# Operand sums beside other products, sums' transfers in two bundles, another order of tables, loads and banks

## The chip, the core and the metric

The kernel runs on one core of a Trainium2 chip. Its engines work side by side, each on its own list of instructions: TensorE (PE) for matrix products into PSUM, VectorE (DVE), ScalarE (ACT) and GpSimd (POOL) for everything between, SyncE (SP) for issuing transfers; POOL issues transfers too. The metric is the time on the device from start to end of one execution, in microseconds, as a median over runs.

## The reference

Two layers, on 512 tokens (S) of width 1024 (D). Each layer mixes the tokens along four branches and then runs a gated feed-forward block:

```python
for l in range(2):
    h = rms_norm(x, g_pre_mix[l])
    # h @ w_in gives all projections: FOX q,k,v and forget gate; dilated q,k,v;
    # retention q,k,v and gate; latents cq (256), ckv (128), kr (32)
    o_a = causal_block_attention(fq, fk, fv, decay=cumsum(log_sigmoid(ff + b_forget)))
    o_b = dilated_attention(dq, dk, dv)
    o_c = silu(rg) * group_norm(retention(rope(rq), rope(rk), rv)) * ret_gn_gain
    o_d = causal_block_attention(MLA: rms_norm(cq) @ w_uq, rms_norm(ckv) @ w_ukv, rope(kr))
    gates = sigmoid(h @ w_gate)                       # 4 x 1024 columns
    merged = sum over the four branches of (o_n @ w_branch[n]) * gates[n]
    x = x + rms_norm(merged @ w_out, g_post_mix)
    h = rms_norm(x, g_pre_ffn)
    x = x + rms_norm((silu(h @ w_ffn_gate) * (h @ w_ffn_up)) @ w_ffn_down, g_post_ffn)
```

The feed-forward width is 2816, 22 blocks of 128. All is float32.

## The kernel before

Activations lie with the features on the 128 partitions and the 512 tokens along the row. A float32 product is made of three faster ones: both operands are split into a high and a low part, and high x high, high x low and low x high are added in PSUM (`mm3`, L528 to L530). The high part of a weight is a cast by ACT (L289, L403), the low part a subtraction by DVE (L290, L404). Weights come from HBM in 512 KB pieces on SP's queue (L258) into three `raw` buffers. Activations are split by `split_to` (L520 the cast, L521 the subtraction; L523 and L524 where a scale goes with it).

PSUM has eight banks in two rotating sets of four, "acc" and "b"; a product takes the next bank of its set, and waits until what was in that bank has been read. SBUF tiles for activations, `a`, rotate in the same way.

The order of the instructions is made at build time. Most of a layer is written as generators, one for the main stage and a list of background ones, and a scheduler then orders each engine's list; only the first block, the ends of the two blocks and the start of a layer (`ordered(True)` to `ordered(False)`) keep the order in which they are written.

A layer runs: `latents` (the four token tiles of cq, ck and the forget gate lie in the four "acc" banks, while the first half of the `dq` product runs in a "b" bank; DVE then reads the latents out at L1213 to L1217); `project` (all projections, with `mla_prepare` and the attentions in the background: transposes of the latents at L893 and L899, then K and Q from `uq` and `ukv`, which are loaded at L872 and L873); `gates`; `out_block`; `ffn`; and between the layers `down_block`.

`gates` goes through the branches; for each it makes the eight gate tiles in four pairs (`dp`): DVE scales (L1299), ACT takes the tanh (L1300), DVE multiplies with the branch's product (L1319), and from the second branch on POOL adds the result to `merged` (L1320). For the last branch (`gi == 3`) `merged` is then split for `out_block`. In the same place `make_sums` starts transfers on POOL's queue that add blocks of the last weight matrix in DRAM: p = a21 + a22, r = a11 + a21, q = p + a11, v = q + a12. Each sum is a copy and an adding transfer, and each waits for the landing of the one that it builds on. A 1x1 transfer from the gate tile holds them back until the gate is there (L360).

`ffn` makes the first four of the 22 blocks (`m`) plainly, then nine groups of two in `quarter_products`: seven products in place of eight, from quarters of the operands, each group in four banks of one set, the sets taking turns. In the last layer `to_tokens` turns the residual to token order in the background (L1726 transposes into "b", L1729 copies out).

`finish` is the last layer's down projection, again seven products (`n` = 0 to 6) in place of eight. Their right operands are the weight blocks and sums, streamed; the left ones are quarters of the hidden tiles `h` or their sums: t1 = difference of halves, t2, t3 and t4 (L1753, L1757, L1783, L1790), each made for 11 blocks of 128. Operands are made three steps ahead (`OPS`), weights two steps (`AHEAD`). The last steps of a product (`k >= LATE`) are held and run for the first bank, then for the second, so that the first can be read out (`after`: copy L1837, adds, square L1815, root L551) while the second fills. Products 0, 4, 5 and 6 share the banks `chain`. The operands of a product are made by

```python
products = (plain(0, h0), plain(FH, h0), of_t1, plain(FH, h1), of_t2, of_t3, of_t4)
beside = {1: make_t1, 3: make_t2}
```

where `of_t3` and `of_t4` compute the sum when the operand is due, and `beside` names what is computed step by step during another product.

## Time and profile before

| | us |
|---|---|
| median of 3 runs | 1693.74 |
| lowest and highest | 1692.67, 1696.91 |
| the profiled execution | 1688.88 |
| its span, first to last instruction | 1687.1 |
| PE busy | 1650.9 |
| DVE, ACT, POOL busy | 1132.2, 851.2, 376.1 |
| mean granted clock of PE | 0.997 |

The span is the time from the first to the last instruction; 1.8 us lie outside of it. "Busy" counts instructions in work, not those that wait. The ends of matrix products are modelled, and neighbouring products overlap in the records: a 512-column product is shown with 0.39 us and the next begins 0.23 us after it. The gap in front of an instruction, and what ended it, is therefore the surest reading.

### The profile page before, as it was taken

Reading aid. Unit: us, or ns where it says so; the run is one execution under the profiler, and the core shown is the slowest. Engines: PE = TensorE matmul, PEld = TensorE weight load, DVE = VectorE, ACT = ScalarE, POOL = GpSimd, SP = SyncE. Lnnn points to the kernel's source line nnn. Section 1 sums busy time; section 2 is a strip of 40 time slices with the busy share of each in tenths; the row PEclk is TensorE's granted clock in tenths of the full one; section 3 lists DMA queues with packets and bytes.
Section 4 is the critical chain, followed back from the end, with each engine's and each line's share of the span. In section 5 each row is a group of like instructions: output and inputs, shape, how many; then the busy total and the mean of one; then the engine's idle time right before and its main releaser. Section 6 shows DMA issues by size and latency. Waiting matters only on the chain.

```text
span 1687.1 us, 26433 instructions
## 1 busy us (share of the span) xinstructions
PE 1650.9 (98%) x9746; PEld 1460.2 (87%) x9746; DVE 1132.2 (67%) x2149; ACT 851.2 (50%) x1680; POOL 376.1 (22%) x404
## 2 busy tenths in 40 slices
PE   9999999999999999999999999999999999999997
PEld 7788888888798999988887888888888989999875
DVE  6667777644569777762286577675445687777987
ACT  6566553323455555553265665533334565555664
POOL 0145333332230000000121453334332300010000
PEclk9999999999999999999999999999999999999998
DMA  5644325776625777343236343257755257775561
GB/s 198 178 107 127 93 82 185 171 191 157 201 82 146 182 184 183 101 152 101 76 128 181 104 130 90 84 176 179 192 142 174 65 150 193 184 186 150 189 238 68
DMA packets 93313, 248.88 MB, mean 148 GB/s; under 512 B 11136, under 2 KB 22656, under 8 KB 93184
## 3 DMA queue, kind: packets, MB, share of 16 engines
q1 hardware_dynamic: 72768, 205.24, 38.8%
q0 software_dynamic: 20416, 41.95, 13.4%
q8 instruction: 77, 1.26, 0.3%
q14 instruction: 52, 0.43, 0.1%
HBM read 220.93 MB, written 31.46 MB: 150 GB/s over the span
## 4 chain that ended last, share of the span: by engine, by line
PE 59%; DVE 5%; ACT 2%; issue 1%; DMA 1%; POOL 1%; DVEq 0%; SPq 0%; ACTq 0%
PE acc L528 8%; PE acc L529 8%; PE acc L530 8%; PE acc L502 4%; PE acc L504 4%; PE acc L503 4%; PE b L504 3%; PE b L503 3%; PE b L502 3%; PE b L1889 1%; PE b L1891 1%; PE b L1890 1%; PE b L751 1%; DVE wlo L290 1%; PE b L671 1%
## 5 line engine op out<-in xcount | busy, mean ns | idle before, releaser
L528 PE MATMUL acc<-a,whi 128*128 128x512 f32 (+1 forms) x1238 | 477.8, 386 | 3.0 <-DVE a L1299 3.0
L530 PE MATMUL acc<-a,wlo 128*128 128x512 f32 (+1 forms) x1238 | 469.0, 379 | 0.0
L529 PE MATMUL acc<-a,whi 128*128 128x512 f32 (+1 forms) x1211 | 458.6, 379 | 0.0
L290 DVE TENSOR_TENSOR wlo<-raw,whi 128x512 fp32r<-128x512 f32 (+3 forms) x398 | 279.0, 732 | 134.1 <-ACT whi L289 133.3
L289 ACT CAST whi<-raw 128x512 fp32r<-128x512 f32 (+3 forms) x398 | 213.0, 576 | 305.8 <-PE acc L529 155.9
L530 PEld LDWEIGHTS acc<-a,wlo 128*128 128x128 f32 x1238 | 233.0, 188 | 44.0 <-issue 0.5
L528 PEld LDWEIGHTS acc<-a,whi 128*128 128x128 f32 x1238 | 233.9, 189 | 42.5 <-ACT whi L289 3.8
L529 PEld LDWEIGHTS acc<-a,whi 128*128 128x128 f32 x1211 | 228.5, 189 | 38.9 <-DVE a L524 0.6
L404 DVE TENSOR_TENSOR wlo<-raw,whi 128x1024 fp32r<-128x1024 f32 x132 | 157.6, 1195 | 71.2 <-ACT whi L403 67.7
L403 ACT CAST whi<-raw 128x1024 fp32r<-128x1024 f32 x132 | 135.4, 1027 | 122.7 <-PE acc L503 51.1
L502 PE MATMUL acc<-a,whi 128*128 128x256 f32 x560 | 158.6, 283 | 1.9 <-DVE a L1638 1.5
L503 PE MATMUL acc<-a,whi 128*128 128x256 f32 x560 | 158.4, 283 | 0.0
L504 PE MATMUL acc<-a,wlo 128*128 128x256 f32 x560 | 158.3, 283 | 0.0
L502 PE MATMUL b<-a,whi 128*128 128x256 f32 x448 | 126.8, 283 | 0.0
L503 PE MATMUL b<-a,whi 128*128 128x256 f32 x448 | 126.8, 283 | 0.0
L504 PE MATMUL b<-a,wlo 128*128 128x256 f32 x448 | 126.8, 283 | 0.0
L1299 DVE TENSOR_TENSOR a<-acc,a 128x512 f32<-128x512 f32 x64 | 44.1, 689 | 111.4 <-PE acc L530 111.4
L520 ACT CAST a<-a 128x512 fp32r<-128x512 f32 (+1 forms) x143 | 77.6, 567 | 74.7 <-DVE a L859 18.0
L333 POOL DMA_DIRECT2D raw<-wts x36 | 31.6, 877 | 350.1 <-DMA raw<-wts 129.0
L502 PEld LDWEIGHTS acc<-a,whi 128*128 128x128 f32 x560 | 107.4, 192 | 2.3 <-ACT whi L403 1.7
L503 PEld LDWEIGHTS acc<-a,whi 128*128 128x128 f32 x560 | 107.5, 192 | 0.1
L504 PEld LDWEIGHTS acc<-a,wlo 128*128 128x128 f32 x560 | 107.4, 192 | 0.0
(280 smaller groups left out, 3237.7 us busy)
## 6 DMA issues: line engine op xcount, KB each, us to landing
raw<-wts SPq DMA_DIRECT2D x257, 512.0 KB, 3.9
raw<-wts POOLq DMA_DIRECT2D x36, 512.0 KB, 6.5
a<-a SPq DMA_DIRECT2D x120, 128.0 KB, 2.3
sums<-wts POOLq DMA_DIRECT2D x30, 512.0 KB, 7.3
raw<-sums SPq DMA_DIRECT2D x20, 512.0 KB, 3.9
raw<-wts SPq DMA_DIRECT2D x35, 256.0 KB, 2.9
sums<-sums POOLq DMA_DIRECT2D x10, 512.0 KB, 4.6
a<-xT SPq DMA_DIRECT2D x16, 256.0 KB, 5.4
```

Of the source, the lines that this page charges most:

```text
L289: todo.append(lambda hi=hi, src=src, n=n: nc.scalar.copy(hi[:, :n], src))
L290: todo.append(lambda hi=hi, lo=lo, src=src, n=n: (lo_engine or nc.vector).tensor_sub(lo[:, :n], src, hi[:, :n].bitcast(F32)))
L403: self.nc.scalar.copy(hi, src)
L404: self.nc.vector.tensor_sub(lo, src, hi.bitcast(F32))
L502: mm(o, hi[:, c], x[k][0], start=first, stop=False, skip_group_check=i in (2, 3, 4, 6))
L503: mm(o, hi[:, c], x[k][1], start=False, stop=False, skip_group_check=i in (2, 3, 4, 6))
L504: mm(o, lo[:, c], x[k][0], start=False, stop=k == 3, skip_group_check=i in (2, 3, 4, 6))
L520: nc.scalar.copy(hi, src)
L528: mm(out, w[0], x[0], start=start, stop=False)
L529: mm(out, w[0], x[1], start=False, stop=False)
L530: mm(out, w[1], x[0], start=False, stop=stop)
L1299: nc.vector.tensor_mul(z, ps, self.rB)
```

## The change

- `make_sums` takes the names of the sums: p and r start at the first pair of gates, q and v at the third. Each sum now has its own 1x1 transfer ahead of it.
- For the last branch DVE, not POOL, adds to `merged`.
- `uq` and `ukv` are loaded at the beginning of `latents`. Both halves of the `dq` product go to "acc", except the one that runs beside the latents. A dummy exponential follows the latents, the forget gate's functions are computed where `running_sum` needs them, and three empty scheduling steps (`yield`) are added.
- In `down_block` two weight subtractions move from step `EA` to step 1.
- The groups of quarter products begin with "b" instead of "acc", and `finish` swaps its sets too.
- In `finish`, t3 is made beside product 2 and t4 beside product 4, as whole tiles; t4 overwrites t2.

```diff
--- before.py
+++ after.py
@@ -346,18 +346,19 @@
         return [self.ap["wts"][self.woff[i + j]:self.woff[i + j + 1]].rearrange("(p n) -> p n", p=128)
                 for j in range(len(LAST_K))]
 
-    def make_sums(self, j, when):
+    def make_sums(self, j, names, when):
 
         dma = self.nc.gpsimd.dma_start
         a11, a12, a21, a22 = (self.block_quarter(n)[j] for n in range(4))
         n = a11.shape[1]
         for name, first, more in (("p", a21, a22), ("r", a11, a21), ("q", None, a11), ("v", None, a12)):
+            if name not in names:
+                continue
             d = self.dram.tile([128, n], F32, tag="%s%d" % (name, j), name="sums")
             self.sums[name, j] = d
             if first is None:
                 first = self.sums["p" if name == "q" else "q", j]
-            else:
-                dma(d[0:1, 0:1], when[0:1, 0:1])
+            dma(d[0:1, 0:1], when[0:1, 0:1])
             dma(d, first, max_dma_last_dim=1024)
             dma(d, more, accum_op=ALU.add, max_dma_last_dim=1024)
 
@@ -849,6 +850,8 @@
         yield
         yield
         yield
+        yield
+        yield
         rb = self.ps("b")
         for t in range(4):
             ts = slice(128 * t, 128 * t + 128)
@@ -866,14 +869,9 @@
     def mla_prepare(self, l, cq, ck, res):
         nc = self.nc
         ident = self.con("ident")
-        uq_raw = [self.a(), self.a()]
-        ukv_raw = self.a()
-        for k in range(2):
-            nc.sync.dma_start(uq_raw[k], self.ap["uq"][l, :, k, :])
-        nc.sync.dma_start(ukv_raw, self.ap["ukv"][l])
-        uq = [self.split(t) for t in uq_raw]
-        yield
-        ukv = self.split(ukv_raw)
+        uq = [self.split(self.up.pop(0)) for _ in range(2)]
+        yield
+        ukv = self.split(self.up.pop(0))
         for p in range(2):
             c = ck[p][:, 0:384].rearrange("p (t c) -> p t c", t=2)
             cs = slice(64 * p, 64 * p + 64)
@@ -914,6 +912,7 @@
                 for p in range(2):
                     self.move(K[h][p][64:128, :], K[0][p][64:128, :])
         self.defer(shared)
+        yield
         yield
         Q = []
 
@@ -1185,6 +1184,9 @@
         cq, ck = [self.a(), self.a()], [self.a(), self.a()]
         z = self.small(16)
         junk = self.a()
+        self.up = [self.a() for _ in range(3)]
+        for t, src in zip(self.up, (self.ap["uq"][l, :, 0, :], self.ap["uq"][l, :, 1, :], self.ap["ukv"][l])):
+            nc.sync.dma_start(t, src)
         w = self.take("dq", 0)
         ps_d = self.ps("b")
         for k in range(KT):
@@ -1225,7 +1227,8 @@
         nc = self.nc
         cq, ck, z, ps_d = self.latents(l, u)
         yield
-        nl = self.forget(z)
+
+        nc.scalar.activation(self.small(1), z[:, 0:1], AF.Exp, scale=0.0)
         self.br = {n: {} for n in range(4)}
         m = {"qk": [], "v": []}
         self.bg.append(("mprep", self.mla_prepare(l, cq, ck, m)))
@@ -1235,7 +1238,7 @@
             q, k, v = [], [], []
             for i in range(2):
                 if ps_d is None:
-                    ps_d = yield from self.fm(nq, u, "b" if kind == DIL else "acc")
+                    ps_d = yield from self.fm(nq, u)
                 q.append(self.queries(self.scaled(ps_d, 0.125)))
                 ps_d = None
                 yield 3
@@ -1244,7 +1247,7 @@
                 yield 3
             yield from self.tm_full(nv, u, 256, lambda t, ps: v.append(self.v_split(ps, self.rT[:, t:t + 1])))
             if kind == FOX:
-                self.bg.append(("forget", self.running_sum(nl)))
+                self.bg.append(("forget", self.running_sum(self.forget(z))))
             self.bg.append(("b%d" % kind, self.lazy_attention(kind, self.heads(q, k), v)))
 
         q, k, v, g = [], [], [], []
@@ -1299,8 +1302,8 @@
                     nc.vector.tensor_mul(z, ps, self.rB)
                     nc.scalar.activation(z, z, AF.Tanh, scale=0.5)
                     ts.append(z)
-                    if d == 0 and dp == 0 and gi > 0:
-                        self.make_sums(3 * l + gi - 1, z)
+                    if d == 0 and dp % 2 == 0 and gi > 0:
+                        self.make_sums(3 * l + gi - 1, ("pr", "qv")[dp // 2], z)
                     yield 3
                 if dp == 0:
                     self.drain("b%d" % n)
@@ -1317,7 +1320,7 @@
                     else:
                         t = ts[d]
                         nc.vector.scalar_tensor_tensor(t, t, 1.0, ps, op0=ALU.add, op1=ALU.mult)
-                        nc.gpsimd.tensor_add(merged[dd], merged[dd], t)
+                        (nc.vector if gi == 3 else nc.gpsimd).tensor_add(merged[dd], merged[dd], t)
                     if gi == 3:
                         merged[dd] = self.split(merged[dd], scale=0.5)
                 yield 12
@@ -1462,10 +1465,10 @@
         squares(1)
         lows.pop(0)()
         lows.pop(0)()
-        at = {0: [lambda: some(g[0], 4), lambda: convert()], 1: [lambda: some(g[0], 4)],
+        at = {0: [lambda: some(g[0], 4), lambda: convert()], 1: [lambda: some(g[0], 4), *(lambda: lows.pop(0)() for _ in range(2))],
               EA: [lambda: sums(1), lambda: some(chain[1], 2), lambda: some(g[0], 4), lambda: some(chain[1], 2),
                    lambda: some(g[0], 4), lambda: some(chain[1], 100), lambda: some(g[0], 100),
-                   lambda: convert(), *(lambda: lows.pop(0)() for _ in range(4))],
+                   lambda: convert(), *(lambda: lows.pop(0)() for _ in range(2))],
               ES: [lambda: start(1), lambda: some(g[1], 4)]}
         wl = []
         for i in range(4):
@@ -1692,7 +1695,7 @@
                     stt(z[1][:, h0], o, -1.0, z[1][:, h0], op0=ALU.mult, op1=ALU.mult)
                     keep(z[1])
 
-            yield from self.quarter_products(ops, ("acc", "b")[g % 2], {
+            yield from self.quarter_products(ops, ("b", "acc")[g % 2], {
                 0: copy(0), 1: copy(1), 2: copy(2), 3: after_v, 4: after_r, 5: after_a12, 6: after_a22})
         self.wi = self.q_end
         return hid
@@ -1739,7 +1742,7 @@
         gout = [self.a(), self.a()]
         for i in range(2):
             nc.sync.dma_start(gout[i], self.ap["gout"][:, 512 * i:512 * i + 512])
-        t1, t2 = [None] * FH, [None] * FH
+        t1, t2, t3 = ([None] * FH for _ in range(3))
         row = lambda k: (k // 2, HALF[k % 2])
 
         def total(dst, k, f):
@@ -1771,29 +1774,28 @@
                 return hi, lo
             return f
 
-        def of_t1(k, nk):
-            return split(t1[k // 2], 256 * nk)
-
-        def of_t2(k, nk):
-            return split(t2[k // 2], 256 * nk)
-
-        def of_t3(k, nk):
-            t = self.a()
-            for i in range(nk):
-                nc.vector.tensor_sub(t[:, HALF[i]], h[FH + k + i][:, h1], h[k + i][:, h1])
-                h[k + i] = None
-            return split(t, 256 * nk)
-
-        def of_t4(k, nk):
-            t = self.a()
-            for i in range(nk):
-                stt(t[:, HALF[i]], t2[k // 2][:, HALF[i]], -1.0, h[FH + k + i][:, h0], op0=ALU.mult, op1=ALU.subtract)
-            t2[k // 2] = None
-            return split(t, 256 * nk)
-
-        products = (plain(0, h0), plain(FH, h0), of_t1, plain(FH, h1), of_t2, of_t3, of_t4)
-
-        beside = {1: make_t1, 3: make_t2}
+        def make_t3(k):
+            total(t3, k, lambda o: nc.vector.tensor_sub(o, h[FH + k][:, h1], h[k][:, h1]))
+            h[k] = None
+
+        def make_t4(k):
+
+            i, hs = row(k)
+            o = t2[i][:, hs]
+            stt(o, o, -1.0, h[FH + k][:, h0], op0=ALU.mult, op1=ALU.subtract)
+
+        def of(t, last):
+            def f(k, nk):
+                src = t[k // 2]
+                if last:
+                    t[k // 2] = None
+                return split(src, 256 * nk)
+            return f
+
+        products = (plain(0, h0), plain(FH, h0), of(t1, False), plain(FH, h1), of(t2, False), of(t3, True),
+                    of(t2, True))
+
+        beside = {1: make_t1, 2: make_t3, 3: make_t2, 4: make_t4}
         todo = deque((f, k, nk) for f in products for k, nk in LAST_K)
         ready = deque()
 
@@ -1802,7 +1804,7 @@
                 f, k, nk = todo.popleft()
                 ready.append(f(k, nk))
 
-        chain, other, late = ([self.ps(t), self.ps(t)] for t in ("b", "b", "acc"))
+        chain, other, late = ([self.ps(t), self.ps(t)] for t in ("acc", "acc", "b"))
         banks = (chain, other, late, late, chain, chain, chain)
         e = {}
         y, xt = {}, {}
```

Three places show what this does to the order. In the first, PE at the start of layer 1 before: the end of the first `dq` product (bank b_9074) and the second one (b_9202). a_87.. are the activations' high and low parts, whi and wlo the weights.

```order
L528 MATMUL b_9074<-a_8775,whi_8992 128x512
L529 MATMUL b_9074<-a_8776,whi_8992 128x512
L530 MATMUL b_9074<-a_8775,wlo_8993 128x512
L528 MATMUL b_9202<-a_8761,whi_9123 128x512
L529 MATMUL b_9202<-a_8762,whi_9123 128x512
L530 MATMUL b_9202<-a_8761,wlo_9124 128x512
```

The same place after the change; b_9250, b_9275 and b_9299 take the transposes of the latents.

```order
L529 MATMUL b_9088<-a_8783,whi_9000 128x512
L530 MATMUL b_9088<-a_8784,whi_9000 128x512
L531 MATMUL b_9088<-a_8783,wlo_9001 128x512
L891 MATMUL b_9250<-ct_79,a_9076 128x128
L891 MATMUL b_9275<-ct_79,a_9076 128x128
L897 MATMUL b_9299<-ct_79,a_9078 128x128
L529 MATMUL acc_9209<-a_8769,whi_9137 128x512
```

The second `dq` product moves from "b" to "acc", and three transposes of the latents come ahead of it. In the second place, PE in layer 1 before, in the first group of quarter products (L502 to L504), 12 of its products behind the last plain one:

```order
L502 MATMUL acc<-a,whi 128x256
L503 MATMUL acc<-a,whi 128x256
L504 MATMUL acc<-a,wlo 128x256
L1726 MATMUL b<-ct,a 128x128 x16
L502 MATMUL acc<-a,whi 128x256
L503 MATMUL acc<-a,whi 128x256
```

After:

```order
L530 MATMUL acc<-a,whi 128x512
L531 MATMUL acc<-a,wlo 128x512
L1729 MATMUL b<-ct,a 128x128 x16
L503 MATMUL b<-a,whi 128x256
L504 MATMUL b<-a,whi 128x256
L505 MATMUL b<-a,wlo 128x256
```

Before, 15 quarter products stood between the last plain product and the 16 transposes; now the transposes follow the last plain product, the group follows them, and both use "b". In the third place, ACT in `finish` before, at the end of product 5 (b_16647 and b_16648 are the two `chain` banks; L551 is the root):

```order
L1837 COPY a_17551<-b_16647 128x512
L1815 ACTIVATE a_17554,sm16_16653<-a_17551 128x512
L1837 COPY a_17581<-b_16648 128x512
L551 ACT_TABLE_LOAD
L551 ACTIVATE sm1_17560<-sm1_17558 128x1
L1815 ACTIVATE a_17584,sm16_16653<-a_17581 128x512
```

After:

```order
L1839 COPY a_17572<-acc_16663 128x512
L1817 ACTIVATE a_17575,sm16_16669<-a_17572 128x512
L404 CAST whi_17627<-raw_17483 128x1024
L552 ACT_TABLE_LOAD
L552 ACTIVATE sm1_17581<-sm1_17579 128x1
L1839 COPY a_17602<-acc_16664 128x512
```

A weight cast, the table load and the root now stand ahead of the second bank's copy.

## Rows read from the trace of the kernel before

**Rows 1.** The page, busy time, share of the span and number of instructions.

```profile
PE 1650.9 (98%) x9746; PEld 1460.2 (87%) x9746; DVE 1132.2 (67%) x2149; ACT 851.2 (50%) x1680; POOL 376.1 (22%) x404
```

**Rows 2.** PE's waits, whole span: line, releaser, us in total, times, longest.

```profile
PE b L697 <- POOL a L690: 4.4, 6, 1.8
...
PE b L528 <- DVE a L524: 3.2, 2, 2.0
PE b L1889 <- ACT a L1837: 3.1, 2, 2.7
PE acc L528 <- DVE a L1299: 3.0, 2, 2.0
PE b L906 <- DVE a L1095: 1.9, 2, 1.7
PE acc L1041 <- DVE wlo L290: 1.6, 1, 1.6
PE acc L502 <- DVE a L1638: 1.5, 1, 1.5
```

**Rows 3.** Timeline, PE and DVE at both layer starts: start, us, engine, line [idle before].

```profile
32.46 0.39 PE L530 MATMUL b<-a,wlo 128*128 128x512 f32 x1
...
34.28 0.47 DVE L1213 TENSOR_SCALAR a<-acc,sm 128x256 f32<-128x256 f32 x1
...
874.31 0.39 PE L528 MATMUL b<-a,whi 128*128 128x512 f32 x1
...
877.87 0.47 DVE L1213 TENSOR_SCALAR a<-acc,sm 128x256 f32<-128x256 f32 x1
```

**Rows 4.** Timeline, PE at the first attention step of each layer.

```profile
84.92 0.33 PE L697 MATMUL b<-ct,a 128*128 128x128 f32 x1 [1.13 <-POOL a L690]
...
930.22 0.33 PE L697 MATMUL b<-ct,a 128*128 128x128 f32 x1 [1.82 <-POOL a L690]
```

**Rows 5.** Timeline, POOL, ACT and PE in layer 0's gates, last branch.

```profile
412.17 0.66 POOL L361 DMA_DIRECT2D sums<-sums  x1 [5.05 <-DMA sums<-wts]
...
414.17 0.63 ACT L523 ACTIVATE a<-a 128x512 fp32r<-128x512 f32 x1 [7.47 <-POOL a L1320]
...
416.27 0.47 PE L528 MATMUL acc<-a,whi 128*128 128x512 f32 x1 [1.05 <-DVE a L1299]
```

**Rows 6.** Timeline, PE and ACT at layer 1's first group of quarter products.

```profile
1382.78 1.93 PE L1726 MATMUL b<-ct,a 128*128 128x128 f32 x16
...
1381.95 4.00 ACT L1729 COPY a<-b 128x512 f32<-128x512 f32 x8
```

**Rows 7.** Timeline, DVE and PE at the end of layer 0's down block.

```profile
850.70 2.11 DVE L290 TENSOR_TENSOR wlo<-raw,whi 128x420 fp32r<-128x420 f32 x4
...
852.40 0.60 PE L599 MATMUL b<-ct,sm 128*128 128x128 f32 x4
```

**Rows 8.** Windows of the finish: busy us (instructions) by engine, granted clock, DMA share, GB/s.

```profile
1595.00:1610.00 15.00, 15.00 (x68) 12.43 (x67) 11.93 (x19) 10.63 (x20) 0.00 (x0) 1.00 0.63 205
...
1626.00:1641.00 15.00, 15.00 (x68) 12.41 (x67) 13.28 (x20) 10.35 (x16) 0.00 (x0) 1.00 0.54 190
...
1660.00:1665.00 5.00, 4.56 (x13) 3.22 (x14) 4.46 (x9) 2.96 (x7) 0.00 (x0) 0.66 0.01 3
```

**Rows 9.** DVE's groups from 1626 to 1679: busy us, mean ns of one, idle before.

```profile
L1790 DVE SCALAR_TENSOR_TENSOR a<-a 128x256 f32<-128x256 f32 x11 | 4.3, 417 | 0.0
```

**Rows 10.** Timeline, ACT at the end of product 5.

```profile
1658.00 1.04 ACT L403 CAST whi<-raw 128x1024 fp32r<-128x1024 f32 x1
...
1662.05 0.63 ACT L1815 ACTIVATE a<-a 128x512 f32<-128x512 f32 x1 [2.01 <-DVE a L1845]
...
1662.68 0.57 ACT L1837 COPY a<-b 128x512 f32<-128x512 f32 x1
1663.26 1.28 ACT L551 ACT_TABLE_LOAD   x1
1664.56 0.20 ACT L551 ACTIVATE sm<-sm 128x1 f32<-128x1 f32 x1
```

## The prediction

> **What bounds the kernel now.** I read the page's busy shares first, then the table of what TensorE (PE) waits for, then the timelines around the longest of those waits. [rows 1]: PE is busy 1650.9 of 1687.1 us. VectorE (DVE) has 67%, ScalarE (ACT) 50%, GpSimd (POOL) 22%. So no other engine is the bound on average; only stretches in which PE stands still can be won, and the edits neither add nor remove a matrix product. [rows 2] name these stretches: seven kinds of wait, 18.7 us together, each at a place that the change touches. A wait costs a little more than the table shows, because the first matrix product behind a wait takes longer too: 0.47 us in [rows 5] against 0.39 to 0.40 at full pace in [rows 3]. I charge 0.2 us for each wait that goes or comes, for the slow first products (an estimate from those two rows).
>
> **The change part by part.** Times are those of the profiled execution.
>
> *Gates, fourth branch.* POOL waits in its own queue for the landing of one sum before it issues the next, and the add into `merged` stands behind that issue: [rows 5] show the issue at 412.17 after 5.05 us, and ACT's conversion L523 at 414.17, idle for 7.47 us until that add (L1320) is done. DVE does the other half of that conversion (L524), and L1299, which frees PE's bank, stands behind it: PE goes on at 416.27, and the two such waits are the 3.0 us of L1299 in [rows 2]. The change puts this add on DVE (eight adds per layer of the size of L1299, some 0.7 us) and splits the sums' transfers in two bundles. DVE waited there for the same conversion, so the adds are hidden. Gain 3.0. The twelve added 1x1 transfers and the second bundle, now at the third pair of gates, block POOL only; the next POOL work in layer 0 follows the last gates, and the adds of the second and third branch are needed one branch later. I cost them at nothing.
>
> *Quarter products' banks.* The first group now opens "b" instead of "acc", which still holds the last gate. In layer 0 the wait on L1638 goes: 1.5. In layer 1 the last 16 transposes (L1726) also need "b". Before, 15 products of the first group stood ahead of them; now they and the group come right behind the last gate product, and both wait for the eight copies in [rows 6], one per 0.5 us from 1381.95. PE would arrive at about 1381, run the transposes as the copies release banks, and start the group when a second set is free, about 1384.5 after 1.9 us of work: between 0.5 and 2.5 us lost, I take 1.8.
>
> *Layer starts.* The up-projection weights of the latents (`uq`, `ukv`) are loaded before the latents instead of behind the first moves, so their splits no longer hold up DVE's L1095 and L524. The four waits on these two lines go: 3.2 + 1.9 = 5.1. But the second `dq` product now goes to "acc", and all four "acc" banks hold the latents until DVE has read them; before, this product ran in "b" and covered that. [rows 3]: the first `dq` product ends its issue at 32.46 in layer 0 and the second latents' tile is ready at 34.28 + 0.47 = 34.75, so 34.75 - 32.69 = 2.1 us of new idle time; in layer 1 from 874.31 to 877.87 + 0.47 = 878.34, that is 4.0 us. A pause of 2.7 us is in the trace, before product 6 of the finish [rows 2], and behind it the granted clock was 0.66 for 5 us [rows 8], between the two levels (1.2 and 2.4 GHz); 4.56 busy us at a third less cost 1.5 us. The 4.0 us pause is longer, so I charge 1.5 there; the 2.1 us pause I charge nothing, since it resembles the 2.0 us one of L524.
>
> *First attention step.* ACT loads the exponential's table and works off late `v` copies before the first exponential; PE waits for it at 84.92 and 930.22, 1.13 + 1.82 = 2.95 [rows 4]. The change loads the table earlier with a dummy operation and moves work out of the way. I take the whole 2.95, with an end of zero, because the forget gate's own exponential and logarithm still stand between the dummy and the first attention step and may load over it. The three empty scheduling steps can shift the rest of L690's waits (4.4 - 2.95 = 1.45 in [rows 2]) either way; I charge nothing.
>
> *Two weight corrections of layer 0's down block.* Two of four DVE subtractions (2.11 us for four [rows 7]) move ahead of the norm's small steps. The wait of 1.6 us on them goes, but the norm's result is 1.06 us later, at about 851.85 instead of 850.78. PE, no longer held, reaches the spread (852.40 in [rows 7]) at 852.40 - 1.6 = 850.8 and waits 1.2.
>
> *Finish.* Today operands t3 and t4 are computed inside products 5 and 6 (counted from 0), where DVE is the busiest; now beside products 2 and 4. The number of operations is the same, 11 of each (t4: [rows 9], 0.417 us each, 4.3 in all). What goes: the 3.1 us on L1837 in [rows 2] and the 1.5 us of low clock [rows 8], 4.6 together. Does it fit in the new place? From 1595 to 1610 DVE is busy 11.93 of 15, and PE has no wait: 4.6 more makes 16.5, 1.5 over. From 1626 to 1641 it is 13.28, of which 3 of t3's steps (1.2) leave: 16.7 with t4, 1.7 over. Operands are made three steps ahead, each step 12 products of 0.227 = 2.7 us, so there are about 8 us of lead to pay this from. I charge nothing, with 3.2 as the other end. What stays: at the end of product 5 ACT does in the new order copy, square, weight cast, table load, root, and only then the second bank's copy, which in the old order stood ahead of the table load. With [rows 10] (copy 0.57, square 0.63, cast 1.04, load 1.28, root 0.20, copy 0.57) and 0.7 for DVE's add of 128x512 (an estimate from the 0.417 of a 128x256 in [rows 9]) that is 5.0 us after the first bank is full. PE has 9 held products and 6 of the next step, 15 x 0.227 = 3.4. So 1.6 us of waiting come back, plus 0.6 for one operand that the new order puts behind a weight subtraction: 2.2.
> [rows 10] show the root 0.02 us behind the end of its table load. The Trainium skill (ScalarE: Activation LUTs, "What ACT_TABLE_LOAD costs") gives 1283 ns for the load and some 1380 ns of drain, 2.66 us for a switch. By it the second copy would come 1.4 us later and the forecast would be 1.4 us higher; the row has the load at the page's 1.28 and no drain behind it, so the row decides.
>
> **Sum.** Gone: gates 3.0, quarter group 1.5, layer starts 5.1, attention 2.95, down block 1.6, finish 4.6 = 18.75. New: quarter group 1.8, layer starts 2.1 + 4.0 + 1.5 = 7.6, down block 1.2, finish 2.2 = 12.8. Net 5.95. Twelve waits go (two gates, one quarter group, four at starts, two in attention, one in the down block, two in the finish), six come (one quarter group, two starts, one down block, two in the finish): six times 0.2 = 1.2. Together 7.2 us. The profiled execution would go from 1688.88 (its span of 1687.1 and 1.8 around it) to 1681.7. It lies 4.9 below the median of the runs shown, 1693.74; the same 7.2 us put the median at 1686.5.
>
> **Rivals.**
> 1. *The waits move instead of going.* The table load stays in front of the first exponential (+2.95), and the finish keeps half of its waits because ACT, with the same conversions and a later copy, sets the pace there (+2.5). For it: the number of table loads per layer is unchanged in the order. Against: ACT's conversions of t3 and t4 then find their input ready, and ACT is at 50% [rows 1]. 7.2 - 5.5 = 1.7 gained: 1692.0.
> 2. *DVE becomes the bound of the finish, and the kernel is slower.* If the lead is used up when product 2 begins, the 1.5 and 1.7 us over reach PE, each wait followed by a low clock (1.5 each), and the finish gives none of its net gain (4.6 - 2.2): 3.2 + 3.0 + 2.4 = 8.6 worse than forecast, 1.4 slower than before: 1695.1. It decides from the point at which DVE is some 8 us behind, products 2 to 4 being the place. Against: PE is busy 15.00 of 15 in both of these windows [rows 8], so the lead is not used up there today.
> 3. *The starts cost nothing.* Other work covers part of the new idle time (the transposes wait one by one) and the clock does not fall: 4.0 + 1.5 of the new 7.6 go, and half of the quarter group's 1.8: 1686.5 - 6.4 = 1680.1.
> 4. *The starts cost it all.* The four waits come back because Q and K products now stand closer to the conversions that they need; 5.1, and 0.8 for four slow first products, 5.9 worse, 1.3 gained: 1692.4. An idle PE arrives later, though, so that old waits shrink by what was lost ahead of them.
>
> **How the numbers follow.** Forecast (1683 to 1688.7): 0.5. Rival 3: 0.15. Rivals 1 and 4: 0.23 together. Rival 2: 0.12. The predicted time is 1686.5. The range reaches down to a little under rival 3's time, 1679.0, and up to rivals 1 and 4, 1692.8; it leaves out rival 2 and a rest below. About 0.3%, 5 us, is what a measurement of this kernel can tell from no change. Faster by more than that, under 1688.7: 0.5 + 0.15 = 0.65. Rivals 1 and 4 and most of rival 2, whose 1695.1 is also within 0.3%, make the middle: 0.29. For a case beyond rival 2, above 1698.8: 0.06.
>
> **What would show it.** In the table of PE's waits: no L1299 and no L1638 (gates, quarter group); L524 and L1095 gone, in their place a pause of PE at 32.7 and one of some 4 us at 874 behind DVE's latents (layer starts), with a lower clock behind the second; the transposes L1729 waiting for copies at 1381; no wait for POOL's L690 at the two first attention steps; in the finish one wait of about 1.6 us at the last product's first step, on the copy behind the table load, and 1.00 as granted clock there. Wrong would make it: waits on DVE's weight subtractions between 1595 and 1645, waits for POOL behind the second bundle of sums, or a first attention step that still waits for the exponential.

## The result and the profile after

The changed kernel takes 1677.64 us (median of 4 runs, 1676.69 to 1679.01) against 1693.28 (4 runs, 1692.67 to 1696.91): a ratio of 0.9904, 95% interval 0.9887 to 0.9921. It is faster, as forecast, but by 15.6 us where I had forecast 7.2, and 1677.64 lies below my range (1679.0 to 1692.8). Five later runs of it gave 1676.66, against 1691.12 for nine runs of the kernel before on the same chip: 14.5 us. Its profiled execution took 1679.01 with a span of 1677.2. Gains of whole kernels are differences of medians; those of single parts below are the ratio (of means) times the median of the kernel before. One of the five executions of a_dve below took 2164.83 us at a mean granted clock of 0.702 and is left out of its ratio. Line numbers of the new kernel are up to 3 higher or, around `mla_prepare`, 1 or 2 lower.

The page and the table of PE's waits of the changed kernel, against [rows 1] and [rows 2]:

```profile
PE 1649.3 (98%) x9746; PEld 1463.0 (87%) x9746; DVE 1130.8 (67%) x2165; ACT 851.0 (51%) x1682; POOL 358.7 (21%) x400
```

```profile
PE b L891 <- DVE a L1215: 4.1, 2, 3.1
...
PE b L858 <- DVE a L848: 2.1, 2, 1.5
PE b L1729 <- ACT a L1732: 1.4, 1, 1.4
...
PE b L1891 <- ACT a L521: 1.1, 1, 1.1
PE b L600 <- DVE sm L562: 1.0, 1, 1.0
PE b L1891 <- ACT a L1839: 1.0, 1, 1.0
...
PE b L698 <- POOL a L691: 0.6, 2, 0.3
...
PE acc L1891 <- ACT a L1839: 0.3, 1, 0.3
```

The busy shares hardly moved; the waits did. Gone are the gates' L1299, the quarter group's L1638, both waits at the starts (L524, L1095), the weight correction in the down block, and most of POOL's L690 (now L691: 4.4 to 0.6). New are L891 at the two starts, L1729 at the last layer's quarter group, L600 in the down block, and two that I had not named at all: L858, and L672 inside the attention (0.6 us in each layer):

```profile
PE b L672 <- DVE ptl L709: 1.1, 2, 0.6
```

**Layer starts** ([rows 3]). The timeline of PE and DVE at the start of layer 1, the window behind it, and PE at the start of layer 0:

```profile
871.55 0.48 DVE L1215 TENSOR_SCALAR a<-acc,sm 128x256 f32<-128x256 f32 x1
...
872.19 0.52 PE L891 MATMUL b<-ct,a 128*128 128x128 f32 x2 [3.09 <-DVE a L1215]
...
873.72 0.63 PE L531 MATMUL acc<-a,wlo 128*128 128x512 f32 x1
874.15 0.63 PE L529 MATMUL acc<-a,whi 128*128 128x512 f32 x1
```

```profile
872.00:877.00 5.00, 4.81 (x16) 3.82 (x17) 5.00 (x19) 2.86 (x5) 0.00 (x0) 0.66 0.04 16
```

```profile
35.75 0.44 PE L891 MATMUL b<-ct,a 128*128 128x128 f32 x2 [1.03 <-DVE a L1215]
```

PE goes on 0.16 us behind the first tile of the latents (871.55 + 0.48 = 872.03). The pause is 3.09 us, and behind it the granted clock of the window is 0.66: products start 0.43 us apart (874.15 - 873.72) where 0.23 is the pace at full speed, the lower of the two levels (1.2 GHz). In layer 0 the pause is 1.03 us.

**Finish** ([rows 8, 10]). PE's two waits at bank changes, ACT in front of each, and the window of the last product:

```profile
1604.10 1.05 ACT L404 CAST whi<-raw 128x1024 fp32r<-128x1024 f32 x1 [1.78 <-issue]
1605.05 1.07 ACT L1839 COPY a<-b 128x512 f32<-128x512 f32 x2
...
1605.68 0.50 PE L1891 MATMUL b<-whi,a 128*128 128x512 f32 x1 [0.99 <-ACT a L1839]
```

```profile
1651.01 0.59 ACT L1839 COPY a<-acc 128x512 f32<-128x512 f32 x1 [0.98 <-PE acc L1893]
...
1654.04 1.28 ACT L552 ACT_TABLE_LOAD   x1
1655.33 0.20 ACT L552 ACTIVATE sm<-sm 128x1 f32<-128x1 f32 x1
1655.44 0.57 ACT L1839 COPY a<-acc 128x512 f32<-128x512 f32 x1
...
1656.06 0.50 PE L1891 MATMUL acc<-whi,a 128*128 128x512 f32 x1 [0.33 <-ACT a L1839]
```

```profile
1655.00:1660.00 5.00, 4.67 (x21) 3.56 (x20) 4.61 (x14) 4.99 (x11) 0.00 (x0) 1.00 0.19 71
```

The long pause before the last product is gone, and the clock there is 1.00. A new wait of 1.0 us stands at 1605.68: a weight cast is ahead of the bank's copies in ACT's list. Three smaller waits of the kernel before, in products 5 and 6, have no counterpart in the new order:

```profile
1647.18 0.50 PE L1889 MATMUL b<-whi,a 128*128 128x512 f32 x1 [0.36 <-ACT a L520]
...
1668.52 0.50 PE L1891 MATMUL b<-whi,a 128*128 128x512 f32 x1 [0.27 <-DVE a L521]
...
1671.24 0.50 PE L1889 MATMUL b<-whi,a 128*128 128x512 f32 x1 [0.16 <-ACT a L520]
```

**Quarter group and down block** ([rows 6, 7]). PE and ACT at the last layer's first quarter group, then DVE and PE at the end of layer 0:

```profile
1375.51 4.00 ACT L1732 COPY a<-b 128x512 f32<-128x512 f32 x8
...
1376.14 2.12 PE L1729 MATMUL b<-ct,a 128*128 128x128 f32 x16 [1.44 <-ACT a L1732]
```

```profile
846.59 0.16 DVE L562 TENSOR_TENSOR sm<-sm,sm 128x2 f32<-128x2 f32 x1
...
846.81 0.71 PE L600 MATMUL b<-ct,sm 128*128 128x128 f32 x4 [1.00 <-DVE sm L562]
```

**Group norm of the retention branch**, the wait that was not foreseen. DVE, POOL and PE in layer 0 of the changed kernel:

```profile
294.70 3.43 DVE L542 TENSOR_TENSOR sm<-sm 128x8 f32<-128x8 f32 x1
298.16 0.17 DVE L543 TENSOR_TENSOR sm<-sm,sm 128x8 f32<-128x8 f32 x1
...
295.18 2.92 POOL L1323 TENSOR_TENSOR a<-a 128x512 f32<-128x512 f32 x2
...
299.41 1.13 PE L858 MATMUL b<-ct,a 128*128 128x128 f32 x8 [1.46 <-DVE a L848]
```

A DVE operation on 8 columns, 0.17 us elsewhere, takes 3.43 and ends at 298.13, 0.03 us behind POOL's two additions to `merged` (295.18 + 2.92 = 298.10). PE waits for what follows it. What brought the two together are most likely the empty scheduling steps, two of which stand in the group norm; of the other edits at the start and in the mixing stage, s_loads, s_exp and a_dqb below rule out the loads, the exponential and the `dq` bank, each by itself. A layer has two such norms. In all nine kernels without these steps the second begins 20.1 to 20.2 us behind the first, and POOL's first addition comes 3.4 to 7.6 us behind its last small operation; in all seven kernels with them it begins 24.5 to 27.4 us behind, and where POOL adds there, it begins between 3.6 us before that operation's end and 1.0 us after it. p_start below has the steps and not the bundles, and DVE is held there too, behind one addition:

```profile
291.84 2.17 DVE L541 TENSOR_TENSOR sm<-sm 128x8 f32<-128x8 f32 x1
...
292.29 1.69 POOL L1322 TENSOR_TENSOR a<-a 128x512 f32<-128x512 f32 x1
```

p_gates has the bundles and not the steps, and no such operation. In the kernels with both, two additions stand in a row, so that DVE is held longer. Neither the steps nor the bundles were taken out of the changed kernel alone.

**Where the time went, by place.** For every matrix product I took the time from its start to the next start, less the pace of its shape (the lower quartile of all of that shape, 0.226 us for 128x512), and summed by place. "Old, mean" is the mean of the profiles of all kernels below that leave this place as it was (6 to 9 profiles); "new, mean" that of the changed kernel and its variants that have this place as changed (4 to 6 profiles).

| place | before | old, mean | new, mean | change of the means | forecast |
|---|---|---|---|---|---|
| gates, last branch, layer 0 | 3.9 | 4.1 | 0.2 | -3.9 | -3.4 |
| first quarter groups | 4.9 | 4.9 | 4.45 | -0.4 | +0.3 |
| layer starts | 9.2 | 10.7 | 9.7 | -1.0 | +2.1 |
| first attention steps | 8.4 | 8.9 | 4.4 | -4.5 | -3.4 |
| down block, end of layer 0 | 2.2 | 2.2 | 1.7 | -0.5 | -0.4 |
| finish | 9.2 | 9.3 | 4.4 | -4.9 | -2.4 |
| sum | 37.8 | 40.1 | 24.85 | -15.2 | -7.2 |

The forecast column holds the prediction's terms, with the 0.2 us of each wait and the low clock put to its place. The sum of the means is of the size of the 14.5 to 15.6 us that were timed; the group norm and all other places are not in it. The tally also counts slow products under a low clock. In nine of the sixteen profiles of this study a stretch of 3.4 us at the lower level stands behind a wait of 1.1 to 1.3 us on a weight subtraction (L530 or L531) at the end of layer 0, just ahead of the start of layer 1 and no work of the change; it is in neither profile that the first comparison rests on.

### The profile page after: what moved, and what is told of

Same layout as the page of the kernel before. It is cut to its first block, busy times and chain, and to the rows that moved or that the text cites. A ratio compares the mean times of both kernels' runs of the same rounds, so it can differ in the third digit from the quotient of the medians.

```text
span 1677.2 us, 26506 instructions
## 1 busy us (share of the span) xinstructions
PE 1649.3 (98%) x9746; PEld 1463.0 (87%) x9746; DVE 1130.8 (67%) x2165; ACT 851.0 (51%) x1682; POOL 358.7 (21%) x400
## 4 chain that ended last, share of the span: by engine, by line
PE 89%; DVE 6%; issue 2%; ACT 1%; DMA 1%; POOL 1%; DVEq 0%; SPq 0%; POOLq 0%
PE acc L529 15%; PE acc L530 15%; PE acc L531 15%; PE b L503 4%; PE b L505 4%; PE b L504 4%; PE acc L505 3%; PE acc L504 3%; PE acc L503 3%; PE b L752 2%; PE b L672 2%; PE b L698 1%; PE acc L1891 1%; PE acc L1893 1%; PE acc L1892 1%
## 5 line engine op out<-in xcount | busy, mean ns | idle before, releaser
L529 PE MATMUL acc<-a,whi 128*128 128x512 f32 (+1 forms) x1254 | 485.5, 387 | 0.0
L531 PE MATMUL acc<-a,wlo 128*128 128x512 f32 (+1 forms) x1254 | 475.2, 379 | 0.0
L530 PE MATMUL acc<-a,whi 128*128 128x512 f32 (+1 forms) x1227 | 465.3, 379 | 0.0
L290 DVE TENSOR_TENSOR wlo<-raw,whi 128x512 fp32r<-128x512 f32 (+3 forms) x398 | 271.9, 713 | 133.4 <-ACT whi L289 132.7
L531 PEld LDWEIGHTS acc<-a,wlo 128*128 128x128 f32 x1254 | 236.3, 188 | 44.7
L529 PEld LDWEIGHTS acc<-a,whi 128*128 128x128 f32 x1254 | 237.1, 189 | 40.0 <-issue 1.0
L530 PEld LDWEIGHTS acc<-a,whi 128*128 128x128 f32 x1227 | 231.9, 189 | 38.9 <-issue 1.0
L503 PE MATMUL b<-a,whi 128*128 128x256 f32 x560 | 158.7, 283 | 0.0
L504 PE MATMUL b<-a,whi 128*128 128x256 f32 x560 | 158.5, 283 | 0.0
L505 PE MATMUL b<-a,wlo 128*128 128x256 f32 x560 | 158.5, 283 | 0.0
L503 PE MATMUL acc<-a,whi 128*128 128x256 f32 x448 | 126.8, 283 | 0.0
L504 PE MATMUL acc<-a,whi 128*128 128x256 f32 x448 | 126.8, 283 | 0.0
L505 PE MATMUL acc<-a,wlo 128*128 128x256 f32 x448 | 126.8, 283 | 0.0
L503 PEld LDWEIGHTS b<-a,whi 128*128 128x128 f32 x560 | 107.5, 192 | 0.2
L504 PEld LDWEIGHTS b<-a,whi 128*128 128x128 f32 x560 | 107.5, 192 | 0.0
L505 PEld LDWEIGHTS b<-a,wlo 128*128 128x128 f32 x560 | 107.5, 192 | 0.0
L521 ACT CAST a<-a 128x512 fp32r<-128x512 f32 (+1 forms) x143 | 76.6, 567 | 51.8 <-DVE a L1094 10.7
```

What stands on the lines that cost most here:

```text
L290: todo.append(lambda hi=hi, lo=lo, src=src, n=n: (lo_engine or nc.vector).tensor_sub(lo[:, :n], src, hi[:, :n].bitcast(F32)))
L503: mm(o, hi[:, c], x[k][0], start=first, stop=False, skip_group_check=i in (2, 3, 4, 6))
L504: mm(o, hi[:, c], x[k][1], start=False, stop=False, skip_group_check=i in (2, 3, 4, 6))
L505: mm(o, lo[:, c], x[k][0], start=False, stop=k == 3, skip_group_check=i in (2, 3, 4, 6))
L521: nc.scalar.copy(hi, src)
L529: mm(out, w[0], x[0], start=start, stop=False)
```

## The four parts, each alone on the kernel before

These four kernels ran on one chip together with 30 runs of the kernel before (1691.25, 1688.05 to 1696.15).

**p_finish**, t3 and t4 beside products 2 and 4:

```diff
...
-        products = (plain(0, h0), plain(FH, h0), of_t1, plain(FH, h1), of_t2, of_t3, of_t4)
-
-        beside = {1: make_t1, 3: make_t2}
...
+        products = (plain(0, h0), plain(FH, h0), of(t1, False), plain(FH, h1), of(t2, False), of(t3, True),
+                    of(t2, True))
+
+        beside = {1: make_t1, 2: make_t3, 3: make_t2, 4: make_t4}
```

> The kernel before with t3 made beside product 2 and t4 beside product 4, nothing else. Theory A (the gain lies where the traces of before and after differ, and is the same in unprofiled runs): the slow starts of matrix products between 1600 and 1680 fall from 9.0 us to about 4 us, 4.8 us faster. Theory B (runs without the profiler hold some 4 to 5 us of waiting in one place of the kernel before that its one profiled run does not show, and this place is the finish): 9 us faster or more, with a trace that shows 5.

Measured: 1686.84 (9 runs), ratio 0.9980, interval 0.9967 to 0.9993: 3.4 us faster. The tally of the finish falls from 9.2 to 4.5 us, with the two waits that the changed kernel has there (1.0 and 0.3). That is theory A.

**p_gates**, the sums' names and bundles, and DVE's additions for the last branch:

```diff
...
-                        self.make_sums(3 * l + gi - 1, z)
+                        self.make_sums(3 * l + gi - 1, ("pr", "qv")[dp // 2], z)
...
-                        nc.gpsimd.tensor_add(merged[dd], merged[dd], t)
+                        (nc.vector if gi == 3 else nc.gpsimd).tensor_add(merged[dd], merged[dd], t)
```

> The kernel before with the sums' transfers in two bundles and the last branch's adds on DVE, nothing else. Theory A (gains as in the traces): the two waits for L1299 go, 3.4 us faster. Theory B (the waiting that the profiled run does not show is here, where POOL waits for transfers to land): 7 to 9 us faster.

Measured: 1687.54 (10 runs), ratio 0.9983, interval 0.9974 to 0.9993: 2.9 us faster. Both waits on L1299 are gone (3.9 to 0.2 in the tally), as in theory A. This profile also has a wait of 4.0 us on L525 at a layer start, a line that this kernel doesn't touch; it is 2.0 at most in [rows 2].

**p_start**, everything at the layer starts and in the mixing stage (early loads, `dq` in "acc", dummy exponential, late forget gate, empty steps):

```diff
...
-            nc.sync.dma_start(uq_raw[k], self.ap["uq"][l, :, k, :])
...
+        for t, src in zip(self.up, (self.ap["uq"][l, :, 0, :], self.ap["uq"][l, :, 1, :], self.ap["ukv"][l])):
+            nc.sync.dma_start(t, src)
...
-                    ps_d = yield from self.fm(nq, u, "b" if kind == DIL else "acc")
+                    ps_d = yield from self.fm(nq, u)
```

> The kernel before with the early loads of uq and ukv, both dq halves in acc, the dummy exponential, the late forget gate and the three empty steps, nothing else. Theory A: old waits of 3.4 us at the starts and 2.95 at the first attention steps go, pauses of 1.2 and 3.3 us with 1.3 us of low clock come, later parts of the mixing stage shift by -1 to +1: about 3 us faster. Theory B (hidden waiting here): 7 us faster or more. My prediction's terms: 5.1 + 2.95 gone, 7.6 come, that is about 0.5 us faster, 1.5 with the slow first products.

Measured: 1686.18 (10 runs), ratio 0.9971, interval 0.9957 to 0.9984: 4.9 us faster, between the two theories and above the 0.5 to 1.5 of my prediction's terms. The attention's tally falls to 4.1; the starts' is 10.7, no better than the mean of the old ones, with both pauses on L890 there (4.1 in sum).

**p_banks**, the quarter groups' and the finish's sets of banks:

```diff
-            yield from self.quarter_products(ops, ("acc", "b")[g % 2], {
+            yield from self.quarter_products(ops, ("b", "acc")[g % 2], {
...
-        chain, other, late = ([self.ps(t), self.ps(t)] for t in ("b", "b", "acc"))
+        chain, other, late = ([self.ps(t), self.ps(t)] for t in ("acc", "acc", "b"))
```

> The kernel before with the sets of banks swapped in the quarter products and the finish, nothing else. Theory A: 1.7 us less in layer 0, a wait of 1.6 us for the transposes in layer 1 in place of 0.5: about 0.5 us faster. Theory B (hidden waiting here): 4 us faster or more.

Measured: 1692.72 (10 runs), ratio 0.9999, interval 0.9985 to 1.0014: no change that can be told, which leaves room for theory A's 0.5 us and none for theory B's 4. One wait goes, the other comes, as the table of waits of this kernel shows (no L1638 is left in it):

```profile
PE b L1726 <- ACT a L1729: 1.4, 1, 1.4
```

The four add to 3.4 + 2.9 + 4.9 = 11.2 us, and 0 for the banks: less than the whole change gives. Each has an uncertainty of some 2 us, and the two weight corrections were not run alone.

## Variants of the changed kernel

Run together, with nine runs of the kernel before (1691.12).

**a_again** is the changed kernel itself, as the measure for the other three.

> The changed kernel itself, unaltered, as the base for the three others on the same chip. Theory A (before's runs differ among themselves because its waits at the layer starts and in the gates depend on when transfers land; the profiled run of before lay at the short end, so the change gains more in the median than the traces show): its runs lie within some 3 us of each other, where before's lie within 8, and the ratio is 0.990 to 0.993. Theory B (before and after scatter alike, and the first measurement's 15.6 us were a matter of few runs): a range of 6 to 8 us and a ratio near 0.9945, the 9.9 us of the traces.

Measured: 1676.66 (5 runs, 1674.89 to 1679.73), ratio 0.9912, interval 0.9898 to 0.9927: the ratio of theory A, not of B. The cause that theory A gives is taken up under "Why the prediction was right in sign and too small". Its profiled span is 1673.1, 4 us shorter than the first profile's: no L858 wait (2.1 us in that profile, 2.4 with the slow first products) and less low clock at the very start of the kernel (the tally of the first 15 us is 3.7 against 5.1).

**a_dqb** puts the second `dq` product back into "b":

```diff
-                    ps_d = yield from self.fm(nq, u)
+                    ps_d = yield from self.fm(nq, u, "b" if kind == DIL else "acc")
```

> The changed kernel with the second dq product back in b. Theory A (the pauses of 1.2 and 3.3 us and the low clock behind the second come from the acc banks that hold the latents, and the early loads of uq and ukv keep the old waits away): both pauses go and no wait for L1095 or L524 above 0.5 us comes back: 4 to 5.8 us faster than the changed kernel. Theory B (my fourth rival: the Q products stand closer to the conversions that they need): the pauses go but 4 us or more of waits on L524 and L1095 return, within 1.5 us of the changed kernel.

Measured: 1672.95 (4 runs, 1671.54 to 1673.72), ratio 0.9887, interval 0.9873 to 0.9901: 3.7 us below a_again. The window behind the place of the pause, and what is left of PE's waits there:

```profile
872.00:877.00 5.00, 5.00 (x30) 4.17 (x29) 5.00 (x12) 2.67 (x6) 1.29 (x1) 1.00 0.30 104
```

```profile
PE b L904 <- DVE a L1094: 0.8, 2, 0.5
```

PE is busy throughout and the clock is 1.00; 0.8 us of the old L1095 come back. The low clock is not gone from this profile, though. It stands earlier, behind a shorter wait at the end of layer 0:

```profile
858.17 0.50 PE L531 MATMUL b<-a,wlo 128*128 128x512 f32 x1 [1.25 <-DVE wlo L290]
```

```profile
857.00:862.00 5.00, 3.83 (x16) 3.21 (x17) 2.88 (x10) 2.39 (x12) 0.00 (x0) 0.74 0.28 105
```

So what the old bank saves is the two pauses (4.1 us less the 0.8). Moving this product is the one part of the change whose cost shows in the times.

**a_dve** gives DVE the additions of all branches, not of the last alone:

```diff
-                        (nc.vector if gi == 3 else nc.gpsimd).tensor_add(merged[dd], merged[dd], t)
+                        nc.vector.tensor_add(merged[dd], merged[dd], t)
```

> The changed kernel with the add into merged on DVE for all branches but the first, so that POOL does none. Theory A (DVE instructions that run beside POOL's adds are stretched, and the new waits at 299.41 and 1136.03 are such a case: a DVE operation on 8 columns took 3.4 us): the waits for L848 go, 1.5 to 2.5 us faster than the changed kernel, and the stretched DVE instructions become few. Theory B (the two waits come from the two added scheduling steps in the group norm): they stay, and 16 more adds of 0.69 us per layer on DVE gain nothing: 0 to 2 us slower than the changed kernel.

Measured: 1677.72 (5 runs, the four in the ratio 1674.88 to 1677.83), ratio 0.9908, interval 0.9892 to 0.9923, which can't be told from a_again's 0.9912. No L858 wait is in its profile, but a_again's has none either, so this run alone decides nothing.

**a_seq** keeps the old sets of banks in the last layer alone:

```diff
-            yield from self.quarter_products(ops, ("b", "acc")[g % 2], {
+            yield from self.quarter_products(ops, (("b", "acc") if xt is None else ("acc", "b"))[g % 2], {
...
-        chain, other, late = ([self.ps(t), self.ps(t)] for t in ("acc", "acc", "b"))
+        chain, other, late = ([self.ps(t), self.ps(t)] for t in ("b", "b", "acc"))
```

> The changed kernel with the old order of banks in the last layer only (quarter products begin with acc, the finish as before in b, b, acc). Theory A: layer 1's transposes wait for nothing (1.6 us gone) and the wait of 0.5 us on the second acc bank returns: 1.1 us faster than the changed kernel. Theory B (the transposes' copies hold PE in either order): same as the changed kernel.

Measured: 1677.28 (1673.77 to 1679.72), ratio 0.9916, interval 0.9902 to 0.9931. In the trace L1729's wait is gone and the place's tally falls from 4.2 to 3.0; 1.2 us can't be told in times that scatter by 6.

## Parts taken apart

Run together, with 16 runs of the kernel before (1691.21).

**s_loads** and **s_exp** split the start. My theory had been that the attention's first steps wait for the exponential's table; the rival was that they wait because the queue of work ahead, held up by the late `uq` and `ukv`, reaches ACT too late. s_loads has the early loads alone, s_exp the dummy exponential and the late forget gate alone:

```diff
-        nl = self.forget(z)
+
+        nc.scalar.activation(self.small(1), z[:, 0:1], AF.Exp, scale=0.0)
...
-                self.bg.append(("forget", self.running_sum(nl)))
+                self.bg.append(("forget", self.running_sum(self.forget(z))))
```

> The kernel before with only the loads of uq and ukv moved into the latents. Theory A (my terms for the starts): the four waits for L1095 and L524 (5.7 us with the slow first products) fall below 1 us together, no pause comes, since dq stays in b, and the waits of the first attention steps (L697 for L690, 3.4 us) stay: 4 to 5 us faster. Theory B (the first attention step hangs on the same chain): those waits go as well, 8 us faster. Theory C (the old waits have another cause too, DVE's own list): half of them stays, 2 to 3 us faster.

> The kernel before with only the dummy exponential and the late forget gate. Theory A (my prediction: the table load and late work on ACT hold up the first exponential): the waits of 1.3 and 2.0 us at the first attention steps go, 3 us faster. Theory B (a table load still stands ahead of the first exponential in the order, three per layer as before): the two waits stay, within 1 us of before; the three empty steps or the earlier loads are then what removes them.

Measured: s_loads 1684.03 (4 runs), ratio 0.9956, interval 0.9940 to 0.9972: 7.4 us faster. s_exp 1690.17 (10 runs), ratio 0.9993, interval 0.9983 to 1.0003: no change that can be told. The tables of waits, s_loads first:

```profile
PE b L697 <- POOL a L690: 2.9, 5, 1.1
...
PE b L901 <- DVE a L1090: 0.9, 2, 0.5
...
PE b L528 <- DVE a L524: 0.6, 2, 0.3
```

```profile
PE b L697 <- POOL a L690: 4.7, 6, 1.8
...
PE b L906 <- DVE a L1095: 2.5, 2, 1.3
...
PE b L528 <- DVE a L524: 1.6, 2, 1.2
```

With the dummy exponential the attention's wait is as long as in [rows 2] (4.7 against 4.4). With the early loads it falls to 2.9, and the starts' two waits from 5.1 to 1.5. So s_exp shows theory B, and s_loads lies between its theories A and B. My theory fell. The changed kernel shows it once more: the table load still stands straight ahead of the first exponential of layer 1, but ends at 918.58, and the first attention step has no wait:

```profile
917.30 1.28 ACT L683 ACT_TABLE_LOAD   x1
918.59 0.40 ACT L683 ACTIVATE a<-a,sm 128x128 f32<-128x128 f32 x1
```

The early loads alone thus take 1.5 of the 3.8 us by which this wait falls (4.4 to 0.6). The rest, with layer 1's 1.1 us, goes only with other edits of p_start. It is not the `dq` bank, since a_dqb has 0.6 us too; the empty steps, or the exponential and the late forget gate once the loads are early, were not taken apart.

**g_dve** has the last branch's additions on DVE, and none of the bundles:

```diff
-                        nc.gpsimd.tensor_add(merged[dd], merged[dd], t)
+                        (nc.vector if gi == 3 else nc.gpsimd).tensor_add(merged[dd], merged[dd], t)
```

> The kernel before with only the last branch's adds on DVE; the sums' transfers stay in one row on POOL. Theory A (the add behind the transfers is what holds PE): both waits for L1299 go, 2.9 us faster, as with both halves. Theory B (the split of the transfers is needed too, since POOL's adds of the third branch come late and DVE now waits for them): a wait of 1 us or more stays at the last branch.

Measured: 1686.90 (5 runs), ratio 0.9970, interval 0.9955 to 0.9984: 5.1 us faster, and both L1299 waits are gone. POOL still sits 6.16 us in its queue for a sum, with nobody behind it, while DVE adds:

```profile
417.91 1.01 POOL L362 DMA_DIRECT2D sums<-wts  x1 [6.16 <-DMA sums<-sums]
...
415.93 0.69 DVE L1320 TENSOR_TENSOR a<-a 128x512 f32<-128x512 f32 x1
```

So one line did the whole of this part. The bundles are not needed for it.

**f_t4** makes t4 beside product 4 and leaves t3 where it was:

```diff
...
-        beside = {1: make_t1, 3: make_t2}
+        beside = {1: make_t1, 3: make_t2, 4: make_t4}
```

> The kernel before with only t4 beside product 4; t3 stays inside product 5. Theory A (the long pause at the start of product 6 comes from t4 and the copies behind its conversion): the pause of 2.9 us and the low clock behind it go, the wait of 0.5 us inside product 5 stays or grows to 2 us because DVE has t3 and t4 there: 2 to 3 us faster. Theory B (t3 in product 5 is what puts DVE behind): the pause at product 6 stays at 2 us or more, less than 1.5 us faster.

Measured: 1687.81 (6 runs), ratio 0.9976, interval 0.9964 to 0.9987: about 4 us faster, as much as p_finish within the uncertainty. The long pause in front of product 6 is gone, as in theory A. The finish's tally is 5.4 against p_finish's 4.5; the difference is a longer wait inside product 5, where t3 is still made late:

```profile
1648.56 0.50 PE L1892 MATMUL b<-whi,a 128*128 128x512 f32 x1 [1.62 <-ACT a L520]
```

t4 carries nearly all of it, t3 one more microsecond.

## Two combinations

**best1** is the changed kernel with the three edits undone that the traces show as a loss: a_dqb, a_dve and a_seq together (their diffs are above). **c_min** is the kernel before with only the edits of s_loads, g_dve and p_finish. Both ran with the kernel before (7 runs, 1691.15).

> The changed kernel with three of its edits undone: the second half of the query dequantizations back with the last feed-forward product (as in a_dqb), every addition of the partial sums on VectorE (as in a_dve), the old order of PSUM banks at the last layer's quarter group (as in a_seq). If VectorE is late at the group norm because GpSimd's additions hold it up, and if the three gains lie behind one another: the waits on L848 (1.4 us in a_dqb's profile) and the 1.6 us at the quarter group are gone, 0.5 us comes back there, so 2 to 3 us below a_dqb, about 1670. If the L848 waits come from something else, they stay and it lands within 1.5 us of a_dqb, about 1672.5.

> The kernel before with five edits only: the early loads of the next layer's first weights (as in s_loads), the fourth group's additions on VectorE (as in g_dve), and the copies and second-bank products of the third and fourth sums beside other products at the end (as in p_finish). Left as before: the dequantizations' place, the one transfer of each group's sums, the exponential's table, the banks, the order of the square roots. If the whole gain lies in these three: 7.4 + 5.1 + 3.4 = 15.9 us below before, about 1675. If the other edits carry a part of it: not lower than 1678, within 1 us of the changed kernel.

Measured: best1 1670.56 (4 runs, 1670.32 to 1670.72), ratio 0.9877, interval 0.9860 to 0.9893: 2.4 us below a_dqb by the medians and 1.7 by the ratios (whose intervals overlap), so the first theory is favoured and not proven by the time. It is the fastest kernel of this study, 20.6 us below the kernel before. Neither L858 nor L1729 is in its table of waits. The group norm's operation in layer 0, which took 3.43 us beside POOL's additions in the changed kernel, is at its length (in a_dqb one of layer 1 took 3.49):

```profile
292.54 0.17 DVE L542 TENSOR_TENSOR sm<-sm 128x8 f32<-128x8 f32 x1
```

What the three edits give apart from one another was not timed in this company; by the traces it is 1.2 for the banks, and 1.2 for L858's wait in a_dqb (its slow first products come on top).

c_min 1676.96 (4 runs, 1674.30 to 1677.68), ratio 0.9912, interval 0.9897 to 0.9926: 14.2 us faster than before, 1 to 2 less than the sum of its three parts, and level with the changed kernel. Neither figure of the expectation was met, 1675 or 1678 and above. The second compared it with the wrong kernel: c_min lacks `dq` in "acc", so a_dqb is the one to set it against. Against that it is 4.0 us slower. So the remaining edits (banks, weight corrections, empty steps, exponential, bundles) are worth some 4 us together, and the changed kernel's `dq` in "acc" gives just that back. The old waits stand in c_min's table:

```profile
PE b L697 <- POOL a L690: 2.5, 5, 1.1
PE acc L1036 <- DVE wlo L290: 1.6, 1, 1.6
```

## Why the prediction was right in sign and too small

The steps that failed are terms of the sum. By the table the starts were off by 3.1 us, the finish by 2.5, the first attention steps by 1.1, and the other three by 1.3 together. Nearly all the places came as forecast; the sizes did not, and for the attention the cause was wrong.

- **Starts: right in kind, the wait taken at the wrong tile.** The pauses came where I put them, with the low clock behind the longer one. But I measured to the second tile of latents (34.28 and 877.87 in [rows 3]); the transposes wait for the first, 0.94 us earlier. I charged 2.1 and 4.0 where 1.0 and 3.1 came, 2.0 too much. The remaining 1.1 lies in the old starts, 10.7 in the mean against 9.2 in the one profile. The waits that go (L524 and L1095) were not longer there, 4.9 on average in the seven profiles that have them against 5.1; what differs is the low clock, of which five of these profiles have six stretches there and that of the kernel before has none. Rival 3 ("the starts cost nothing") would have had -3.4 for this place, and the clock did fall.
- **Finish: what goes was set too low.** I counted as gone the 3.1 us on L1837 and 1.5 of low clock, and they went. But the tally shows 9.2 lost there before: three waits on casts and operands in products 5 and 6 too, 0.3 to 0.5 each with the slow product behind them, which I left out since each is small. With the other slow products in this stretch they are some 1.8 more than in the new order. Of the 2.2 put back, 0.5 came, and a wait of 1.0 at 1605.68 that I had not seen. That these two come near the 2.2 is luck. My 5.0 us for the second bank's copy is exact (from 1651.01 to 1655.44 + 0.57 = 1656.01), and so is the absence of a drain: the root starts 0.01 us behind the table load's end. What was mis-sized there is PE's cover: it worked for 4.6 us before it needed that bank, not 3.4, because products of two further steps stood ahead of it (21 products in the trace), not of one (15).
- **First attention steps: size near, cause wrong.** I took 2.95, with the slow first products 3.4; it was 4.5. I named the exponential's table load as the thing that moves. It didn't move, and the dummy exponential alone changed nothing. The early loads alone take 1.5 us of the wait; what takes the rest stays open. Rival 1 tied its loss to that load staying in place, so it was argued from the same error.
- **Gates: right**, 3.9 against 3.4, and by DVE's additions alone.
- **Empty steps, put at nothing.** I let them shift only the attention's waits. Most likely it is they that put the second group norm some 4 to 7 us later, beside POOL's additions. That is 2.4 us in the first profile and none in a_again's. The bundles, which I also put at nothing, make two of these additions stand in a row.
- **Quarter groups and down block: right** in mechanism and within 0.7 and 0.1 us.
- **From the profile to the median.** I carried the 7.2 us of one execution over as if the profiled run stood for all. The profiled execution took 1688.88; over 30 runs of the kernel before the median was 1691.25, from 1688.05 up. It was one of the shortest: the old starts, attention steps and gates cost 21.5 us there and 23.7 on average, 2.2 more. The waits that the change removes there were not short in it (L524, L1095, L690 and L1299, 12.5 us against 12.3 on average). What it lacked is low clock: in these three places it has none, where the eight other profiles in which one of them is old have ten stretches of 3.4 us. The times point the same way: of 62 runs of the kernel before, the four with the lowest mean clock (0.993) took 1693.4 to 1696.2 and the one with the highest (0.999) 1688.7, though the shortest, 1688.05, had 0.996. The profile of the changed kernel was one of the longer of its kind. That is why the two first spans differ by 9.9 us where the times differ by 14.5 to 15.6. So theory A of a_again had the number, and the landing of transfers, its cause, is not shown for most of it.
- The remaining rival, DVE as the bound of the finish (2), did not come: no wait on a weight subtraction stands between 1595 and 1645. Nor did the four old waits come back (4).

## What to carry to other kernels

Add up all that an engine loses at a place, by its start-to-start times, before pricing what goes there: waits below a microsecond made the difference at the finish. One profile is one draw of the waits, and of the low clock behind them; take several before a forecast carries it to the median. An early load and one addition taken off a queue that waits for transfers were worth more than any reordering of tables and banks, and a product moved to the other bank set cost what several of those gave.
